# Hi tiles at 64 and lo tiles at 32 bytes modulo 128 from the weights, with the substitution's blocks zeroed earlier

## The chip, the cores and the metric

The kernel runs on one core of one Trainium2 chip. The metric is the device time of one execution, in microseconds (us); lower is better. One nanosecond (ns) is a thousandth of that. The engines are TensorE (PE; its weight loads are PEld), VectorE (DVE), ScalarE (ACT), GpSimd (POOL), and SyncE (SP), which here only issues DMA transfers. Each engine, and each issuing queue, works through its own instructions in program order.

## The reference

Two transformer blocks over 256 positions of width 1024, in float32. The part that the change touches is the first block's gated delta rule, whose chunked form needs the inverse of a unit lower triangular matrix for each of 16 pairs of chunk and head:

```python
def first_block(x, ...):
    h = rmsnorm(x, norm_mix_g[l]); proj = h @ w_in[l]
    y_a = short_conv_branch(bg, cg, xv, conv_a_w[l]) @ w_a_out[l]
    y_b = gdn_branch(q, k, v, z, a, b, ...) @ w_b_out[l]
    x = x + (sigmoid(ga) * y_a + sigmoid(gb) * y_b) @ w_o[l]
    x = x + conv_ffn(rmsnorm(x, norm_ffn_g[l]), w_up[l], ffn_conv_w[l], w_down[l])
    return rmsnorm(x, norm_final_g)

def gated_delta_rule_chunked(q, k, v, g, beta):
    decay = exp(where(tril, G[..., :, None] - G[..., None, :], -inf))   # G = cumsum(g)
    L = where(strict, einsum('bnhid,bnhjd->bnhij', k * beta, k) * decay, 0)
    sol = triangular_solve(eye + L, concat([v * beta, k * beta * exp(G)]), lower=True)
    ...                                            # state recurrence over the chunks

def second_block(x, ...):        # dilated attention and retention, gated; then
    x = x + square(relu(rmsnorm(x) @ w_up)) @ w_down
```

## The kernel before

Every dense product is made in three float32r matmuls. A float32 matrix is split into a hi part (rounded by ACT) and a lo part (the rest, subtracted by DVE); weights become the tiles `H` and `L`, the other operand a pair such as `Hh`, `Hl`. The product is hi·H + lo·H + hi·L (`dense`, line 334, which groups all products of one kind: eight matmuls with hi and `H`, eight with lo and `H`, eight with hi and `L`). In `fm_job` the weights are the loaded operand of 128 columns and the pair is the moving operand of 256 columns. In `tm_jobs` and `down2_job` it is the other way round: the pair is loaded, and 512 columns of weights move.

Weights come in jobs of 1 MB, loaded by SP into one of three `raw` buffers (line 316; three jobs ahead), and each job is two units. For unit n the program order is: one step of the running evacuations and side programs (`evs`, `auxes`; each is a Python generator, and a `yield` in it puts what follows it one unit later), the split of unit n+2 (`do_split`: ACT writes `H`, DVE writes `L`), then the matmuls of unit n, then another step of the side programs. So a side program's yields set where its instructions stand in the order of every engine.

Side programs that matter here: `gates` (a softplus series of small DVE operations on 16 columns) leads into `gdn_decay` (row sums on PE, then a decay matrix `gam`, broadcast from memory by two SP transfers, lines 501 and 502) and into `gdn_main`. There `U` is made and sent to memory (`scr`), and read back as 64 rows of 32x32 blocks (`blk` and `eb`, the two halves of tile `ebd`). `subst` inverts the blocks, 31 steps of two operations each, the first eight on DVE, the others on POOL, then writes the inverse and its transpose to memory, and scatters them back as diagonal blocks of `Em` and `Dm` (line 614, half from POOL's queue, half from SP's), tiles that must be zero elsewhere. `sub_ok` then lets `gdn_main` go on with the matmuls of line 663, which read `Dm` and `U`.

Where tiles lie: the pools are laid out one behind the other. `H` and `L` (4,096 bytes each) begin at multiples of 128 bytes. The 15 buckets of 8,192 bytes that hold all large tiles, hi and lo tiles among them, begin at a multiple of 128 too (`LINE_PAD` sees to it), and so do the four `mid` tiles (`mh`, `ml`) of the feed-forward parts. Taken modulo 256 the buckets' distance from `H` and `L` is 0 and that of the `mid` tiles is 128. Ahead of the first job stand dummy matmuls on zeros (`WARM`); they read the moving operand at 48, 56, 64 and 80 bytes (modulo 256) beyond the loaded one, eight matmuls each.

Of the kernel before, what the change touches and what calls it, by code (L numbers as in the profile page):

```python
# [7 lines left out]
F32R = mybir.dt.float32r  # L8
I32 = mybir.dt.int32
# [10 lines left out]
LINE_PAD = 8  # L20
HL_BUFS = 3
W_BUFS = 6
WARM = ([(0, 0, 512, 0)] * 11 + [(128 * i, 1024 + d, 256, i % 2) for d in (12, 14, 16, 20) for i in range(8)])
# [5 lines left out]
GAM_Y = 4  # L29
# [5 lines left out]
SC_Z = 4  # L35
# [63 lines left out]
def _build(tc, nc, A, ACT, DVE, POOL, PE, SP, raw_p, hl_p, c_p, b_p, t_p, m_p, s_p, d_p, x_p):  # L99
# [6 lines left out]
    free_tags = [f"b{i}" for i in range(N_BUCKETS)][::-1]  # L106
    tag_of = {}

    def alloc(shape, dt=F32, what="bk"):
        if not free_tags:  # L110
            raise RuntimeError(f"no bucket for {what} at {cur}: {len(tag_of)}")
        tag = free_tags.pop()
        t = b_p.tile([128] + list(shape), dt, tag=tag, name=nm(what))
        tag_of[id(t)] = (tag, t)
        return t

    def free(*ts):
        for t in ts:
            free_tags.insert(0, tag_of.pop(id(t))[0])
# [92 lines left out]
    cst("pad", [128, LINE_PAD])  # L212
# [31 lines left out]
    Hh = alloc([8, 256], F32R, "Hh")  # L244
# [184 lines left out]
    def gates():  # L429
# [123 lines left out]
    def gdn_main():  # L553
# [27 lines left out]
        def subst():  # L581
# [17 lines left out]
            gd["Em"], gd["Dm"] = alloc([16, 128], what="Em"), alloc([16, 128], what="Dm")  # L599
# [46 lines left out]
        rsqrt(rq, sq, 16, dve=True)  # L646
        rq2 = cst("rq2", [128, 16])
# [127 lines left out]
        Oh, Ol = alloc([8, 256], F32R, "Oh"), alloc([8, 256], F32R, "Ol")  # L775
# [42 lines left out]
    def bg_evac(p):  # L818
        def go(box):
            if p == 0:  # L820
                S["ya"] = (alloc([8, 256], F32R, "yah"), alloc([8, 256], F32R, "yal"))
# [160 lines left out]
    def up_evac(m, gate):  # L982
        def go(box):
# [16 lines left out]
            else:  # L1000
# [7 lines left out]
                mh = m_p.tile([128, 2, 256], F32R, tag="mh", name=nm("mh"))  # L1008
                ml = m_p.tile([128, 2, 256], F32R, tag="ml", name=nm("ml"))
# [325 lines left out]
    def ret_main():  # L1335
# [69 lines left out]
        orr = [(alloc([8, 256], F32R, "orh"), alloc([8, 256], F32R, "orl")) for _ in range(2)]  # L1405
# [128 lines left out]
    def up2_evac(m):  # L1534
        def go(box):
# [5 lines left out]
            mh = m_p.tile([128, 2, 256], F32R, tag="mh", name=nm("mh"))  # L1541
            ml = m_p.tile([128, 2, 256], F32R, tag="ml", name=nm("ml"))
# [123 lines left out]
```

## Time and profile before

| | |
|---|---|
| time, median of 3 runs (lowest, highest) | 1152.12 us (1150.99, 1152.6) |
| the profiled execution: its time, its span | 1150.97 us, 1149.2 us |
| granted TensorE clock, mean over the span | 0.991 of full speed |
| busy: PE, PEld, DVE, ACT, POOL | 98%, 93%, 65%, 51%, 21% |
| HBM read | 191.68 MB, 168 GB/s over the span |

The span runs from the first to the last instruction of the profiled execution; the time has 1.77 us more around it. Matmuls are pipelined: each lasts about 280 ns, but the next one starts long before it ends, so the rate of PE is read from the distance of starts, not from durations or the busy share. The granted clock has two levels, 2.4 GHz (1.00) and 1.2 GHz (0.50); a figure between them is a mean over a stretch.

### The profile page before, as it was taken

What the parts mean: (1) busy time and instruction counts of PE and PEld (TensorE: products, weight loads), DVE (VectorE), ACT (ScalarE), POOL (GpSimd) and SP (SyncE); (2) the same over time, 40 slices, a digit from 0 to 9 for tenths busy, and PEclk for the clock granted to TensorE, in tenths of its full rate; (3) what the DMA queues carried; (4) which work ended last, traced back from release to release, by engine and by line L of the source; (5) the groups of instructions that cost most, each with busy time, mean ns of one, the idle gap of its engine ahead of it and who ended that gap; (6) DMA issues with size and microseconds to landing.
All of it is one profiled execution on the core that took longest, in us unless ns stands there. A gap on an engine that the chain in (4) does not pass through costs nothing.

```text
span 1149.2 us, 20224 instructions
## 1 busy us (share of the span) xinstructions
PE 1127.2 (98%) x8340; PEld 1073.6 (93%) x8340; DVE 750.5 (65%) x1033; ACT 586.0 (51%) x944; POOL 241.7 (21%) x245
## 2 busy tenths in 40 slices
PE   9899897999999999999999999999999999999998
PEld 8899897999999999999878899889999999899997
DVE  4957984344577987778854566556685558655554
ACT  6776253256554444444678554555474445444442
POOL 2565696010401221222200500001340001000000
PEclk9999998999999999999999999999999999999999
DMA  8455366243554555555575544453436555555552
GB/s 258 147 164 186 111 193 174 75 146 112 182 186 150 181 188 183 192 178 178 183 250 190 184 146 147 139 191 113 163 129 220 184 184 168 176 191 189 190 187 74
DMA packets 155087, 194.82 MB, mean 170 GB/s; under 512 B 5678, under 2 KB 132005, under 8 KB 154740
## 3 DMA queue, kind: packets, MB, share of 16 engines
q1 hardware_dynamic: 153888, 191.57, 51.1%
q0 software_dynamic: 912, 1.43, 0.5%
q8 instruction: 65, 1.06, 0.4%
q10 hardware_dynamic: 196, 0.54, 0.1%
q14 instruction: 26, 0.21, 0.0%
HBM read 191.68 MB, written 1.84 MB: 168 GB/s over the span
## 4 chain that ended last, share of the span: by engine, by line
PE 84%; POOL 5%; DVE 4%; ACT 3%; DMA 2%; issue 2%; POOLq 0%; DVEq 0%; ACTq 0%
PE d L334 63%; PE x L334 13%; POOL bt L146 2%; POOL ebd L146 2%; DVE L L146 2%; ACT jk L143 1%; ACT H L143 1%; DVE w L149 1%; DMA Dm<-scr 1%; POOL gam L146 1%; PE x L663 0%; PE x L1181 0%; PE x L1206 0%; DMA scr<-U 0%; DMA xtm<-in_x_dram 0%
## 5 line engine op out<-in xcount | busy, mean ns | idle before, releaser
L146 DVE TENSOR_TENSOR L<-raw,H 128x1024 fp32r<-128x1024 f32 x354 | 443.2, 1258 | 256.8 <-ACT H L143 253.2
L143 ACT ACTIVATE H<-raw 128x1024 fp32r<-128x1024 f32 (+1 forms) x355 | 369.9, 1053 | 205.2 <-PE d L334 152.4
L334 PE MATMUL d<-Hh,L 128*128 128x256 f32 x576 | 82.2, 286 | 6.2 <-DVE L L146 6.2
L334 PE MATMUL d<-Hh,H 128*128 128x256 f32 x576 | 85.6, 292 | 0.7 <-ACT H L143 0.7
L334 PE MATMUL d<-nh,H 128*128 128x256 f32 x608 | 85.9, 283 | 0.0
L334 PE MATMUL d<-nl,H 128*128 128x256 f32 x608 | 85.7, 283 | 0.0
L334 PE MATMUL d<-nh,L 128*128 128x256 f32 x608 | 85.7, 283 | 0.0
L334 PEld LDWEIGHTS d<-Hh,L 128*128 128x128 f32 x576 | 74.7, 193 | 7.4 <-DVE L L146 7.4
L334 PE MATMUL d<-Hl,H 128*128 128x256 f32 x576 | 81.2, 284 | 0.0
L334 PEld LDWEIGHTS d<-nh,H 128*128 128x128 f32 x608 | 79.2, 191 | 1.2
L334 PEld LDWEIGHTS d<-nh,L 128*128 128x128 f32 x608 | 78.6, 192 | 0.0
L334 PEld LDWEIGHTS d<-nl,H 128*128 128x128 f32 x608 | 78.5, 192 | 0.0
L334 PEld LDWEIGHTS d<-Hh,H 128*128 128x128 f32 x576 | 75.2, 194 | 1.4 <-ACT H L143 0.9
L334 PEld LDWEIGHTS d<-Hl,H 128*128 128x128 f32 x576 | 74.9, 193 | 0.0
L334 PE MATMUL d<-H,x2h 128*128 128x512 f32 x208 | 56.9, 396 | 1.0 <-ACT H L143 1.0
L334 PE MATMUL d<-x2h,H 128*128 128x256 f32 x384 | 55.8, 288 | 0.0
L334 PE MATMUL d<-H,x2l 128*128 128x512 f32 x208 | 55.7, 390 | 0.0
L334 PE MATMUL d<-L,x2h 128*128 128x512 f32 x208 | 55.7, 390 | 0.0
L334 PE MATMUL d<-x2h,L 128*128 128x256 f32 x384 | 53.9, 283 | 0.0
L334 PE MATMUL d<-x2l,H 128*128 128x256 f32 x384 | 53.9, 283 | 0.0
L334 PEld LDWEIGHTS d<-x2h,H 128*128 128x128 f32 x384 | 49.8, 190 | 0.6
L334 PEld LDWEIGHTS d<-x2h,L 128*128 128x128 f32 x384 | 49.5, 191 | 0.0
(402 smaller groups left out, 1922.8 us busy)
## 6 DMA issues: line engine op xcount, KB each, us to landing
raw<-in_w_in_dram SPq DMA_DIRECT2D x86, 1024.0 KB, 5.1
raw<-in_w_up_dram SPq DMA_DIRECT2D x38, 1024.0 KB, 5.3
raw<-in_w_down_dram SPq DMA_DIRECT2D x27, 1024.0 KB, 4.8
raw<-in_w_proj_b_dram SPq DMA_DIRECT2D x8, 1024.0 KB, 5.1
raw<-in_w_a_out_dram SPq DMA_DIRECT2D x4, 1024.0 KB, 6.1
raw<-in_w_b_out_dram SPq DMA_DIRECT2D x4, 1024.0 KB, 5.3
raw<-in_w_o_dram SPq DMA_DIRECT2D x4, 1024.0 KB, 6.0
raw<-in_w_out_dram SPq DMA_DIRECT2D x4, 1024.0 KB, 5.2
```

Source lines behind the costliest of these rows:

```text
L143: ACT.activation(out=out, in_=in_, func=func, **kw)
L146: eng.tensor_tensor(out=out, in0=a, in1=b, op=op)
L149: DVE.scalar_tensor_tensor(out=out, in0=in0, scalar=scalar, in1=in1, op0=op0, op1=op1)
L334: PE.matmul(out, lhsT=x if swap else w, rhs=w if swap else x, start=first and ps == 0, stop=last and ps == group[-1] and group is (order o ...
```

## The change

Four of the 15 buckets become 8,320 bytes long, and hi tiles (`alloc_hi`) start 32 bytes into one of those. `LINE_PAD` goes, and small constants are reshuffled, so that every bucket starts 32 modulo 128 from the weights. Lo tiles and all else in buckets thus lie at 32, hi tiles at 64 modulo 128. Modulo 256 a hi tile lies at 64 or 192 beyond `H` and `L`, a lo tile at 32 or 160, depending on the bucket. `mh` and `ml` lie at 32 modulo 128 in the first block and at 0 in the second (`pair`). The dummy matmuls move at 32 or 64 instead of 48 to 80.

```diff
+    def alloc_hi(what):
+        tag, long, t = bucket(F32R, what, True)
+        v = t[:, 8 * long:8 * long + 2048].rearrange("p (a b) -> p a b", b=256)
...
+    def pair(what):
+        d = 24 * ("x2" in S)
+        return m_p.tile([128, 544], F32R, tag=what, name=nm(what))[:, d:d + 512].rearrange("p (a b) -> p a b", b=256)
...
-    cst("pad", [128, LINE_PAD])
...
-    Hh = alloc([8, 256], F32R, "Hh")
+    Hh = alloc_hi("Hh")                 # likewise x2h, nh, Oh, yah, mxh, orh, yh
```

`subst` allocates and zeroes `Em` and `Dm` at its head instead of behind the substitution. The two yields that stood there are gone, and `SC_Z` grows by two, so that line 663 stays at the unit where it was, while the scatter stands two units earlier.

```diff
-SC_Z = 4
+SC_Z = 6
...
-            for _ in range(3):
-                yield
+            gd["Em"], gd["Dm"] = alloc([16, 128], what="Em"), alloc([16, 128], what="Dm")
+            for k in ("Em", "Dm"):
+                POOL.memset(gd[k], 0.0)
+                yield
+            yield
...
-            POOL.memset(gd["Em"], 0.0)
-            yield
-            POOL.memset(gd["Dm"], 0.0)
-            yield
```

The softplus series gets two more yields and `GAM_Y` falls from 4 to 2: `gam` is made from row sums that stand two units later, and is read at the same unit as before. The reciprocal root `rq` on DVE, which ran as one block of nine small operations, is spread over three units:

```diff
-GAM_Y = 4
+GAM_Y = 2
...
-            if k in (2, 4):
+            if k in (1, 2, 4, 5):
...
-        rsqrt(rq, sq, 16, dve=True)
+        a = tmp("nw16", (16,))
+        DVE.tensor_scalar(out=rq.bitcast(I32), in0=sq.bitcast(I32), scalar1=-0.5, scalar2=float(0x5F3759DF), op0=MUL, op1=ADD)
+        for _ in range(3):
+            tt(DVE, a, rq, rq, MUL)
+            stt(a, a, -0.5, sq, MUL, MUL)
+            stt(rq, a, 1.5, rq, ADD, MUL)
+            yield
```

POOL's order at the end of the substitution, before (`scr` is memory, the DMA rows are issues on POOL's queue):

```order
L146 TENSOR_TENSOR ebd_1290<-ebd_1290,bt_1951 64x31
L600 DMA scr_1284<-ebd_1290 64x1024
L601 COPY ebd_1290<-ebd_1290 64x1024
L602 DMA scr_1285<-ebd_1290 64x1024
L603 MEMSET Em_1992 128x2048
L605 MEMSET Dm_1993 128x2048
L608 MEMSET P_2062 128x2048
L614 DMA Em_1992<-scr_1284 32x16x32 x2
L614 DMA Dm_1993<-scr_1285 32x16x32 x2
L146 TENSOR_TENSOR w_2094<-w_2094,w_2095 128x2x255
```

And POOL's order at the head of the substitution, of the change:

```order
L601 DMA ebd_1289<-scr_1282 64x1024
L604 MEMSET ebd_1289 64x1024
L605 MEMSET ebd_1289 64x32
L608 MEMSET Em_1341 128x2048
L608 MEMSET Dm_1342 128x2048
L168 TENSOR_TENSOR bt_1583<-ebd_1289 64x207
```

Two of the three memsets ahead of the scatter stand now between the read of the blocks and POOL's first step; the rest of POOL's order is the same.

SP's order around the scatter, before and then of the change (`raw` rows are weight loads of 1 MB):

```order
L316 DMA raw_2002<-in_w_in_dram 128x8x256
L316 DMA raw_2068<-in_w_a_out_dram 128x8x256
L614 DMA Em_1992<-scr_1284 32x16x32 x2
L614 DMA Dm_1993<-scr_1285 32x16x32 x2
L316 DMA raw_2146<-in_w_a_out_dram 128x8x256
```

```order
L337 DMA raw_2004<-in_w_in_dram 128x8x256
L633 DMA Em_1341<-scr_1283 32x16x32 x2
L633 DMA Dm_1342<-scr_1284 32x16x32 x2
L337 DMA raw_2075<-in_w_a_out_dram 128x8x256
L337 DMA raw_2145<-in_w_a_out_dram 128x8x256
```

The first load of `w_a_out` now stands behind the scatter instead of ahead of it.

DVE's order of the change where `rq` is made (`nw` and `grr` are its small operations, `keep` and `w` belong to the convolution, `L` is the split; before, all nine rows on `nw` and `grr` stood in one block ahead of `w`):

```order
L666 TENSOR_SCALAR grr<-gsum 128x16
L168 TENSOR_TENSOR nw_1700<-grr 128x16
L171 SCALAR_TENSOR_TENSOR nw_1700<-nw_1700,gsum 128x16
L171 SCALAR_TENSOR_TENSOR grr<-nw_1700,grr 128x16
L168 TENSOR_TENSOR w_1711<-d_1637,keep_1631 128x512
L175 TENSOR_SCALAR keep_1713<-w_1711,prm 128x256 x2
L168 TENSOR_TENSOR L_1717<-raw_1500,H_1716 128x1024
L171 SCALAR_TENSOR_TENSOR keep_1713<-w_1711,prm,keep_1713 128x255 x2
L171 SCALAR_TENSOR_TENSOR keep_1713<-w_1711,prm,keep_1713 128x254 x2
L168 TENSOR_TENSOR nw_1700<-grr 128x16
```

Six of the nine now stand behind the next `L`. PE's order differs only in the row sums of `gates`, which stand two units later.

## Rows read from the trace of the kernel before

**Rows 1.** The page: busy time of each engine (share of the span, instructions), and the engines' shares of the chain of work that ended last.

```profile
PE 1127.2 (98%) x8340; PEld 1073.6 (93%) x8340; DVE 750.5 (65%) x1033; ACT 586.0 (51%) x944; POOL 241.7 (21%) x245
PE 84%; POOL 5%; DVE 4%; ACT 3%; DMA 2%; issue 2%; POOLq 0%; DVEq 0%; ACTq 0%
```

**Rows 2.** PE in order of time, in steady stretches: start in us, time from the first start to the last end, line, operation, out<-moving and loaded operand, shape, count.

```profile
318.29 1.12 PE L334 MATMUL d<-Oh,H 128*128 128x256 f32 x8
...
328.85 1.12 PE L334 MATMUL d<-Oh,L 128*128 128x256 f32 x8
...
389.24 1.11 PE L334 MATMUL x<-mh,H 128*128 128x256 f32 x8
...
394.94 1.12 PE L334 MATMUL d<-nh,H 128*128 128x256 f32 x8
...
599.89 1.07 PE L334 MATMUL d<-H,x2h 128*128 128x512 f32 x4
...
610.77 1.07 PE L334 MATMUL d<-H,x2h 128*128 128x512 f32 x4
...
1000.84 1.10 PE L334 MATMUL x<-H,mh 128*128 128x512 f32 x4
...
1003.63 1.11 PE L334 MATMUL d<-nh,H 128*128 128x256 f32 x8
```

**Rows 3.** PE in order of time during the dummy matmuls, in stretches cut so that a row begins with the second of the eight at one distance (48, 56, 64 and 80 bytes in turn); then the first matmuls behind them, of which the last row is 16 transposes with 128 moving columns.

```profile
6.28 0.99 PE L271 MATMUL d<-warm 128*128 128x256 f32 x7
...
7.22 1.00 PE L271 MATMUL d<-warm 128*128 128x256 f32 x7
...
8.18 0.99 PE L271 MATMUL d<-warm 128*128 128x256 f32 x7
...
9.12 1.00 PE L271 MATMUL d<-warm 128*128 128x256 f32 x7
9.96 0.27 PE L250 MATMUL d<-cmats,prr 128*128 128x128 f32 x1
10.07 1.91 PE L282 MATMUL x<-cmats,jk 128*128 128x128 f32 x16
```

**Rows 4.** PE's groups by line, names and shape: count, busy us, mean ns of one, idle time before.

```profile
L334 PE MATMUL d<-nl,H 128*128 128x256 f32 x608 | 85.7, 283 | 0.0
L334 PE MATMUL d<-Hl,H 128*128 128x256 f32 x576 | 81.2, 284 | 0.0
L334 PE MATMUL d<-x2l,H 128*128 128x256 f32 x384 | 53.9, 283 | 0.0
L334 PE MATMUL d<-orl,H 128*128 128x256 f32 x128 | 18.0, 283 | 0.0
L334 PE MATMUL d<-yal,H 128*128 128x256 f32 x64 | 10.1, 307 | 0.0
```

**Rows 5.** The wait for the scatter. First, busy us (and count) of each engine by stretch, with the granted clock, the DMA share and GB/s; then PE in order of time, with the idle time before it and what ended it.

```profile
178.00:187.00 9.00, 1.48 (x13) 1.27 (x11) 2.06 (x4) 5.13 (x11) 6.25 (x8) 0.80 0.98 263
187.00:192.00 5.00, 4.60 (x21) 4.63 (x22) 5.00 (x7) 1.77 (x4) 4.13 (x2) 0.50 0.43 127
...
187.40 3.65 PE L663 MATMUL x<-Dm,U 128*128 128x64 f32 x16 [7.92 <-DMA Dm<-scr]
```

**Rows 6.** POOL in order of time around the substitution.

```profile
112.83 0.98 POOL L583 MEMSET ebd<- 64x1024 f32 x1
...
122.96 0.59 POOL L146 TENSOR_TENSOR bt<-ebd 64x207 f32<-64x207 f32 x1 [8.94 <-DVE ebd L146]
...
167.75 1.11 POOL L146 TENSOR_TENSOR ebd<-ebd,bt 64x31 f32<-64x31 f32 x1
...
172.69 1.82 POOL L603 MEMSET Em<- 128x2048 f32 x1
174.43 1.82 POOL L605 MEMSET Dm<- 128x2048 f32 x1
176.18 1.82 POOL L608 MEMSET P<- 128x2048 f32 x1
...
179.26 1.29 POOL L614 DMA_DIRECT2D Dm<-scr  x2
```

**Rows 7.** Transfers between 160 and 200 us (count, KB each, median us from issue to landing), and SP's queue in order of time.

```profile
raw<-in_w_a_out_dram SPq DMA_DIRECT2D x4, 1024.0 KB, 6.1
...
Dm<-scr POOLq DMA_DIRECT2D x2, 64.0 KB, 7.4
...
163.06 0.37 SPq L316 DMA_DIRECT2D raw<-in_w_a_out_dram  x1
174.54 0.88 SPq L614 DMA_DIRECT2D Em<-scr  x2
```

**Rows 8.** ACT's first instruction behind the stall, in order of time, with its idle time and what ended it.

```profile
181.87 0.63 ACT L143 ACTIVATE w<-w 128x512 f32<-128x512 f32 x1 [10.35 <-POOL w L146]
```

**Rows 9.** Two more stretches in which PE was short of work, in the columns of rows 5.

```profile
46.00:50.00 4.00, 1.73 (x14) 1.53 (x14) 3.90 (x8) 1.72 (x3) 1.42 (x2) 1.00 0.00 0
...
135.00:139.00 4.00, 1.60 (x14) 1.40 (x13) 3.90 (x8) 0.00 (x0) 3.69 (x5) 1.00 0.08 25
```

**Rows 10.** SP's issue of `gam`, and the first DVE operation that reads it.

```profile
58.47 0.34 SPq L502 DMA_DIRECT2D gam<-gs  x1
...
70.91 1.28 DVE L146 TENSOR_TENSOR gam<-gam,cmats 128x512 f32<-128x512 f32 x2
```

More of the change, by code (lines that the diff above doesn't have):

```diff
@@ L19 @@
 N_BUCKETS = 15
-LINE_PAD = 8
+N_LONG = 4
 HL_BUFS = 3
 W_BUFS = 6
-WARM = ([(0, 0, 512, 0)] * 11 + [(128 * i, 1024 + d, 256, i % 2) for d in (12, 14, 16, 20) for i in range(8)])
+WARM = ([(0, 0, 512, 0)] * 11 + [(128 * (i % 8), 1024 + (8 if i in (8, 9, 18, 19, 20, 21) else 16), 256, i % 2) for i in range(32)])
 NEG = -1.0e30
@@ L104, in nm, with bucket @@
         return f"{s}{uid[0]}"
-    free_tags = [f"b{i}" for i in range(N_BUCKETS)][::-1]
+    free_tags = {False: [f"b{i}" for i in range(N_BUCKETS - N_LONG)][::-1], True: [f"l{i}" for i in range(N_LONG)][::-1]}
     tag_of = {}
-    def alloc(shape, dt=F32, what="bk"):
[L110 to L115, printed above, removed]
+    def bucket(dt, what, long):
+        if not free_tags[long]:
+            long = not long
+        if not free_tags[long]:
+            raise RuntimeError(f"no bucket for {what} at {cur}: {[v[2] for v in tag_of.values()]}")
+        tag = free_tags[long].pop()
+        return tag, long, b_p.tile([128, 2080 if long else 2048], dt, tag=tag, name=nm(what))
+    def alloc(shape, dt=F32, what="bk"):
+        tag, long, t = bucket(dt, what, False)
+        n = int(np.prod(shape))
+        v = t[:, 0:n]
+        if len(shape) == 2:
+            v = v.rearrange("p (a b) -> p a b", b=shape[1])
+        elif len(shape) == 3:
+            v = v.rearrange("p (a b c) -> p a b c", b=shape[1], c=shape[2])
+        tag_of[id(v)] = (tag, long, what, v)
+        return v
+    def alloc_hi(what):
+        tag, long, t = bucket(F32R, what, True)
+        v = t[:, 8 * long:8 * long + 2048].rearrange("p (a b) -> p a b", b=256)
+        tag_of[id(v)] = (tag, long, what, v)
+        return v
+    def pair(what):
+        d = 24 * ("x2" in S)
+        return m_p.tile([128, 544], F32R, tag=what, name=nm(what))[:, d:d + 512].rearrange("p (a b) -> p a b", b=256)
     def free(*ts):
         for t in ts:
-            free_tags.insert(0, tag_of.pop(id(t))[0])
+            tag, long = tag_of.pop(id(t))[0:2]
+            free_tags[long].insert(0, tag)
     def tmp(tag, shape=(2, 256), dt=F32, bufs=None):
@@ L774, in gdn_main @@
         yield
-        Oh, Ol = alloc([8, 256], F32R, "Oh"), alloc([8, 256], F32R, "Ol")
+        Oh, Ol = alloc_hi("Oh"), alloc([8, 256], F32R, "Ol")
         while "z_ok" not in S:
@@ L820, in go @@
             if p == 0:
-                S["ya"] = (alloc([8, 256], F32R, "yah"), alloc([8, 256], F32R, "yal"))
+                S["ya"] = (alloc_hi("yah"), alloc([8, 256], F32R, "yal"))
             u = tmp("w", bufs=W_BUFS)
@@ L1007, in go @@
                     yield
-                mh = m_p.tile([128, 2, 256], F32R, tag="mh", name=nm("mh"))
-                ml = m_p.tile([128, 2, 256], F32R, tag="ml", name=nm("ml"))
+                mh = pair("mh")
+                ml = pair("ml")
                 split_act(mh, ml, md)
@@ L1026, in x2_evac @@
         free(*S["xf"])
-        S["x2"] = (alloc([8, 256], F32R, "x2h"), alloc([8, 256], F32R, "x2l"))
+        S["x2"] = (alloc_hi("x2h"), alloc([8, 256], F32R, "x2l"))
         oh, ol = S["x2"]
@@ L1404, in ret_main @@
             yield
-        orr = [(alloc([8, 256], F32R, "orh"), alloc([8, 256], F32R, "orl")) for _ in range(2)]
+        orr = [(alloc_hi("orh"), alloc([8, 256], F32R, "orl")) for _ in range(2)]
         def out_split(h):
@@ L1540, in go @@
             yield
-            mh = m_p.tile([128, 2, 256], F32R, tag="mh", name=nm("mh"))
-            ml = m_p.tile([128, 2, 256], F32R, tag="ml", name=nm("ml"))
+            mh = pair("mh")
+            ml = pair("ml")
             split_act(mh, ml, md)
```

9 lines of the change are left out of this document (4 added, 5 removed).

## The prediction

> **What bounds the kernel now.** I read the page's shares first: PE is busy 98% of the span and carries 84% of the chain of work that ended last; POOL comes next with 5% [rows 1]. So two things can move the time: the rate of matmuls, and the stretch in which PE waits for POOL's substitution.
>
> The rate I took from PE in order of time, as distance from start to start. With `Oh` moving, 88 matmuls of 256 columns (eleven groups of eight from 318.29) take 10.56 us, 120.0 ns each. The 16 transposes behind the dummy matmuls load 128 columns each as well and start (1.91 - 0.27)/15 = 109.3 ns apart [rows 3], so the load of weights alone does not set the 120. With `mh` moving, which lies 128 bytes elsewhere modulo 256, 48 take 5.70 us: 118.75 ns. With 512 columns of `H` moving, the twelve groups of four before 610.77 take 10.88 us, 226.7 ns each with `x2h` loaded; twelve matmuls with `mh` and `ml` loaded take 2.79 us, 232.5 ns [rows 2]. The same form of work goes at different rates, and place is one thing that differs between them, though order is another.
>
> The dummy matmuls show place by itself. From the second of eight at one distance to the second at the next: 0.94 us at 48 bytes (117.5 ns each), 0.96 at 56 (120.0), 0.94 at 64 (117.5); the last seven at 80 take 0.84 us (120.0) [rows 3]. Starts are given to 0.01 us, so each figure is good to 1.3 ns.
>
> The largest single stall is at 179 us: PE does 1.48 us of work in 9 us, then line 663 starts at 187.40, released by the scatter into `Dm`. The granted clock behind it is half, 0.50 from 187 to 192 [rows 5].
>
> **The change part by part: the substitution.** POOL ends the last step at 168.86, then writes, copies, and zeroes `Em`, `Dm` and `P`, three memsets of 1.82 us in a row, and only then issues the scatter [rows 6]. The `Dm` pieces from POOL's queue take 7.4 us to land [rows 7], which gives the release at 187.4. The change takes two of the three memsets out of this chain: 3.64 us. Their new place costs nothing: POOL has zeroed `ebd` by about 114.0 and then idles until 122.96, because DVE does the first eight steps; two memsets from 114.0 end at 117.7, with 5.3 us to spare [rows 6]. Without that cover they would be in the same chain and the gain would be nothing.
>
> Who else profits: ACT stood idle for 10.35 us because a convolution's addition was queued on POOL behind the memsets and the scatter [rows 8]. It too starts 3.64 us earlier, and with it the split of the unit behind line 663, so that unit does not become the next wait.
>
> SP's queue is what the change loads more. SP reached its scatter at 174.54; the load of `w_a_out` had gone ahead of it at 163.06 [rows 7]. Now this load waits behind SP's scatter. That scatter waits for the two writes to memory, not for memsets any more, so I expect it at about 172 and 175, and the load at about 176 instead of 163. With 6.1 us to land it is there at 182. ACT, whose first instruction behind the idle time moves from 181.87 to 178.2, has other work for some 2 us and then wants it, so the split is some 2 us late; PE wants it only behind the first 16 matmuls of line 663, which took 3.65 us [rows 5]. Hidden, with a margin of about 2 us.
>
> The chain may also begin earlier. DVE's small operations starved PE twice: from 46 to 50 us it was busy for 1.73 of 4 us, from 135 to 139 for 1.60 of 4, while DVE was busy for 3.90 in both [rows 9]. The change spreads these operations, so that six of the nine at the second place stand behind the next `L` instead of ahead of it. What PE wins at the second place, up to 2.4 us, is lost again in the wait at 179, since POOL's steps have begun by then and do not follow PE. What it wins at the first place, up to 2.3 us, comes ahead of the chain's begin and moves it, unless POOL's own queue holds it. Nothing to 3 us (with a little from faster matmuls); I take 1.5. Against it stands `gam`: issued at 58.47, read first at 70.91 [rows 10]. Two units of PE are some 6 us, so it is issued at about 65 and, at the 6.1 us of a 1 MB load [rows 7], lands at 71. That is just in time; a wait of up to 1 us on DVE is possible and is in that 1.5.
>
> Sum here: 3.64 + 1.5 = 5.1 us. Bounds: 2.6 (the memsets alone, and `gam` late by 1) and 8 (no stall left).
>
> **The matmuls.** Only those behind 190 us count, because the faster ones ahead of it run into the same wait. Lo parts moving over `H`: 608 + 576 + 384 + 128 in four families [rows 4], and 64 each in four smaller ones, of which `yal` is shown: 1,952. Ahead of 190 us stand 24 jobs of 16, that is 384. So 1,568 lo matmuls remain, and twice as many with hi, 3,136.
>
> Hi at 64 bytes: the dummy row says 117.5 against 120.0, 2.5 ns less [rows 2, 3]. The two starts are rounded, the eight are few and work on zeros, and two thirds of the hi tiles (`Hh`, `x2h`, the last `nh`) lie at 192 and not at 64 modulo 256, which no row shows. I take 2.0; bounds are nothing and 2.5. 3,136 x 2.0 = 6.3 us.
>
> Lo at 32 or 160: no row shows either. The nearest rows are 117.5 (48 and 64) and 120.0 (56, 80 and zero), so from nothing to 2.5 ns; in the middle, 1.2: 1,568 x 1.2 = 1.9 us. `mh` and `ml` in the first block move from 118.75 to a place with the same bounds: no change. Where 512 columns move, the second block's `mid` tiles fall half on distance zero and half on 128; if the 5.8 ns between the two rows of 512 columns come from place alone, half of 384 matmuls save 1.1 us. The 624 with `x2h` and `x2l` loaded go to places without a row; if they lose a third of that, 1.9 ns, it is 1.2 us. I set both against each other at nothing.
>
> Sum: 8.2 us. Of that I keep nine tenths, 7.4, since PE still waits here and there for splits that a faster PE meets sooner. Bounds: nothing, and 3,136 x 2.5 + 1,568 x 2.5 = 11.8.
>
> The Trainium skill speaks against this part. Its page "TensorE: Matmul & The Clock Gate" (Step-by-step: what each phase is for) says that PE has two independent SBUF read ports and that loading the next weights takes no read bandwidth from the running matmul; by it the place of a tile is indifferent and the sum would be 5.1 us alone. The rows disagree at least with the rate that goes with it (256 columns at 120.0 ns, against 109.2 by the formula of its section Back-to-back issue gap, an estimate), so I give that rival below less than the rows.
>
> **How it adds up.** 5.1 + 7.4 = 12.5 us. The profiled execution took 1150.97 us (1149.2 of span and 1.8 around it) and would take 1138.5. It was the fastest of the runs shown; against the median of 1152.1 the same sum gives 1139.6. I predict 1139.
>
> **The rivals.**
> - *Place does nothing.* If the difference in the dummy rows is rounding and the order of reads, the hi and lo matmuls stay at 120.0 and only the substitution gains: 1152 - 5 = 1147. For it: each dummy row has seven or eight matmuls. Against: `mh` at 118.75 over 48.
> - *Place does more.* If 32 bytes bring lo half-way to the transposes' 109.3, to 114.6 ns, lo gains 8.5 us instead of 1.9, and with a stall that vanishes the time is about 1130.
> - *The scatter eats its gain.* Three `raw` loads are now free to go in one run right behind SP's scatter, while POOL's scatter is under way. If its landing grows from 7.4 by the 3.64 us won, only the rest remains: about 1143.
> - *Slower.* A place can cost: 512 columns take 232.5 at one and 226.7 at another [rows 2]. If hi at 192 pays those 5.8 ns, the 2,100 or so such matmuls behind 190 us cost 12.2 us, against 5.1 and some 3.5 won elsewhere: 1155. It decides from about 4.1 ns per matmul on. No row of 256 columns lies above 120, which speaks against it.
>
> **How the numbers follow.** Chances: the forecast 0.62 (its own range 1133 to 1144), place does nothing 0.16, place does more 0.09, the scatter eats its gain 0.08, slower 0.05. The range of 1131 to 1147.5 leaves out the slower case, part of "does more" and the upper edge of "nothing". A change of under 0.2% (2.3 us) can't be told from none here. The second to fourth cases are all faster by more than that in their middle; with their edges: faster 0.91, same 0.05, slower 0.04.
>
> **What the profile of the change would show.** Groups of eight with hi moving start 0.94 us apart, with lo 0.95 (now 0.96 for both); if both stay at 0.96, the second term is wrong. On POOL one memset stands between the second write and the scatter, and two lie in the idle time behind 114 us; line 663 starts at about 182, released by the same scatter, and its wait is still some microseconds long with a half clock behind it, because PE arrives earlier. The stretch about 136 us shows no starved PE. The forecast fails if hi at 192 differs from hi at 64, if DVE's first steps slow down beside the two memsets, if the load of `w_a_out` lands behind 186 and becomes the wait, or if DVE waits for `gam`.

## The result and the profile after

| | before | after |
|---|---|---|
| time, median of 4 runs each, taken together | 1152.3 us | 1131.18 us (1129.97 to 1132.15) |
| ratio | | 0.9818 [0.9801, 0.9835] |
| the profiled execution: time, span | 1150.97, 1149.2 us | 1132.15, 1130.4 us |
| start of the matmuls that wait for `Dm` (line 663, now 688) | 187.40 us | 182.34 us |
| from there to the last start on PE | 957.5 us | 943.7 us |

The change wins 21 us, 1.8%. I had forecast 1139 us, with a range of 1131 to 1147.5; the time lies just inside its lower edge. In the profiled executions the span is 18.8 us shorter: 5.1 us lie ahead of the matmuls on `Dm`, as forecast, and 13.8 us behind them, where I had 7.4.

Line numbers behind the head of the file are 19 to 25 higher than before. From the page of the changed kernel, busy time and the chain that ended last, to hold against [rows 1]:

```profile
PE 1107.6 (98%) x8340; PEld 1051.7 (93%) x8340; DVE 755.6 (67%) x1033; ACT 584.9 (52%) x944; POOL 242.9 (21%) x245
PE 82%; POOL 4%; DVE 2%; ACT 2%; issue 1%; DMA 1%; DVEq 0%; ACTq 0%; POOLq 0%
```

The bound is the same: PE, busy for 98% of a shorter span. The wait for the scatter, to hold against [rows 5 to 7]: POOL in order of time; the transfers from 160 to 200 us (count, KB each, median us from issue to landing); SP's queue; the matmuls that wait; and two stretches (length, then busy time and count of PE, PEld, DVE, ACT, POOL, granted clock, DMA share, GB/s).

```profile
112.81 1.82 POOL L608 MEMSET Em<- 128x2048 f32 x1
114.56 1.82 POOL L608 MEMSET Dm<- 128x2048 f32 x1
121.70 0.59 POOL L168 TENSOR_TENSOR bt<-ebd 64x207 f32<-64x207 f32 x1 [5.32 <-DVE ebd L168]
...
167.42 1.18 POOL L168 TENSOR_TENSOR ebd<-ebd,bt 64x31 f32<-64x31 f32 x1
172.42 1.83 POOL L627 MEMSET P<- 128x2048 f32 x1
174.18 1.34 POOL L633 DMA_DIRECT2D Em<-scr  x2
175.51 1.29 POOL L633 DMA_DIRECT2D Dm<-scr  x2
...
Em<-scr POOLq DMA_DIRECT2D x2, 64.0 KB, 2.7
Dm<-scr POOLq DMA_DIRECT2D x2, 64.0 KB, 4.8
...
175.11 0.83 SPq L633 DMA_DIRECT2D Dm<-scr  x2
176.04 13.38 SPq L337 DMA_DIRECT2D raw<-in_w_a_out_dram  x4
...
182.34 3.65 PE L688 MATMUL x<-Dm,U 128*128 128x64 f32 x16 [6.65 <-DMA Dm<-scr]
185.75 2.06 PE L355 MATMUL d<-yah,H 128*128 128x256 f32 x8
...
178.00:187.00 9.00, 4.66 (x22) 4.69 (x23) 1.90 (x3) 5.07 (x10) 2.52 (x3) 0.62 1.05 323
187.00:192.00 5.00, 5.00 (x32) 5.00 (x32) 5.00 (x8) 3.52 (x6) 3.97 (x2) 0.66 0.54 172
```

The two memsets stand in POOL's idle time, as forecast, and one is left ahead of the scatter. PE still waits 6.65 us, and the granted clock about the wait is 0.62 and 0.66 on the mean, between the two levels (from 182 to 187 us it is 0.50, the lower one). The loads of `w_a_out` now stand behind SP's scatter and start at 176.04, half a microsecond after POOL's into `Dm`. POOL's scatters land faster than before: 2.7 and 4.8 us against some 7.4.

The rate of matmuls, to hold against [rows 2]: PE in order of time in two steady stretches.

```profile
330.80 1.07 PE L355 MATMUL d<-Oh,H 128*128 128x256 f32 x8
331.70 1.10 PE L355 MATMUL d<-Ol,H 128*128 128x256 f32 x8
332.64 1.08 PE L355 MATMUL d<-Oh,L 128*128 128x256 f32 x8
333.56 1.10 PE L355 MATMUL d<-mxh,H 128*128 128x256 f32 x8
334.50 1.10 PE L355 MATMUL d<-mxl,H 128*128 128x256 f32 x8
335.44 1.10 PE L355 MATMUL d<-mxh,L 128*128 128x256 f32 x8
336.38 1.10 PE L355 MATMUL d<-mxh,H 128*128 128x256 f32 x8
...
599.98 1.08 PE L355 MATMUL d<-H,x2h 128*128 128x512 f32 x4
600.90 1.10 PE L355 MATMUL d<-H,x2l 128*128 128x512 f32 x4
601.83 1.08 PE L355 MATMUL d<-L,x2h 128*128 128x512 f32 x4
```

With `Oh` and its neighbours moving, groups of eight started 0.96 us apart [rows 2]. Now `Oh` with `H` takes 0.90 us (112.5 ns each), `Ol` 0.94, `Oh` with `L` 0.92, and all three groups of `mx` 0.94. `Oh` lies 192 bytes modulo 256 beyond the weights, `mxh` 64. With 512 columns the groups of four take 0.92 and 0.93 us, against (610.77 - 599.89)/12 = 0.907 before.

Summed from start to start over all matmuls behind the wait (what exceeds 130 ns, or 245 with 512 columns, is put down as idle; "`x2h`, `x2l` loaded" and "`mid` loaded" are the two kinds with 512 moving columns):

| matmuls behind the wait | count | ns before | ns after | won, us | forecast, us |
|---|---|---|---|---|---|
| hi moving | 3,136 | 120.1 | 116.7 | 10.7 | 6.3 |
| lo moving | 1,568 | 120.1 | 117.4 | 4.3 | 1.9 |
| `mid` tiles and `oab` moving | 624 | 118.9 | 117.0 | 1.2 | 0 |
| 512 columns, `mid` loaded | 383 | 232.4 | 230.0 | 0.9 | 0 |
| 512 columns, `x2h`, `x2l` loaded | 624 | 228.0 | 231.5 | -2.2 | 0 |
| idle and the rest | | | | -1.1 | -0.8 |
| sum | | | | 13.8 | 7.4 |

By place, the 1,920 hi matmuls at 192 bytes went from 120.0 to 115.7 ns, the 1,216 at 64 from 120.1 to 118.1 (modulo 256, as all distances here).

### The profile page after: what moved, and what is told of

It reads as the page before. It is cut to its first block, busy times and chain, and to the rows that moved or that the text cites. A ratio compares the mean times of both kernels' runs of the same rounds, so it can differ in the third digit from the quotient of the medians.

```text
span 1130.4 us, 20225 instructions
## 1 busy us (share of the span) xinstructions
PE 1107.6 (98%) x8340; PEld 1051.7 (93%) x8340; DVE 755.6 (67%) x1033; ACT 584.9 (52%) x944; POOL 242.9 (21%) x245
## 4 chain that ended last, share of the span: by engine, by line
PE 82%; POOL 4%; DVE 2%; ACT 2%; issue 1%; DMA 1%; DVEq 0%; ACTq 0%; POOLq 0%
PE d L355 61%; PE x L355 13%; POOL ebd L168 2%; POOL bt L168 2%; DVE L L168 1%; ACT H L165 1%; DMA Dm<-scr 1%; ACT jk L165 1%; PE x L688 0%; PE x L1206 0%; PE x L1231 0%; PE x L690 0%; ACT w L165 0%; PE x L1265 0%; PE x L691 0%
## 5 line engine op out<-in xcount | busy, mean ns | idle before, releaser
L355 PE MATMUL d<-Hh,L 128*128 128x256 f32 x576 | 79.7, 281 | 8.0 <-DVE L L168 8.0
L355 PE MATMUL d<-Hh,H 128*128 128x256 f32 x576 | 81.6, 284 | 0.7 <-ACT H L165 0.7
L355 PEld LDWEIGHTS d<-Hh,L 128*128 128x128 f32 x576 | 72.1, 188 | 10.1 <-DVE L L168 10.0
L355 PEld LDWEIGHTS d<-Hh,H 128*128 128x128 f32 x576 | 71.7, 188 | 1.1 <-ACT H L165 1.0
L355 PEld LDWEIGHTS d<-Hl,H 128*128 128x128 f32 x576 | 72.5, 188 | 0.0
L165 ACT ACTIVATE w<-w 128x512 f32<-128x512 f32 (+1 forms) x35 | 21.7, 619 | 53.2 <-POOL w L168 22.0
```

The source lines that it names most:

```text
L165: ACT.activation(out=out, in_=in_, func=func, **kw)
L355: PE.matmul(out, lhsT=x if swap else w, rhs=w if swap else x, start=first and ps == 0, stop=last and ps == group[-1] and group is (order o ...
```

## The experiments

The theory after the result: the change has two parts that add up, places (13.8 us) and substitution (5.1), and the place term was too small because hi at 192 runs faster than the row at 64 from which I took it. Rivals: the substitution wins more than line 663 shows; the spreading of DVE's operations does it.

Every run stood beside the kernel before, and "less" and the ratios are against that. Its median was 1150.93 us for the first three runs, 1152.11 for all at 192, all at 64 and hi alone, 1152.18 for the two with hi at 192 and lo at 160 or 32, and 1151.18 for the last two. The two runs with many dummy matmuls are single executions, read for the rates alone.

**Places alone.** The kernel before with the tiles of the change; `subst`, its yields and DVE's operations as before. Since tiles are then allocated in another order, five lo tiles fall into other buckets than in the change: `Ol`, `mxl`, one of the two `orl` and the last `nl` lie at 32 instead of 160, `yl` at 160 instead of 32. All hi tiles lie as in the change.

> The kernel before with the new places alone (hi tiles, lo tiles, the `mid` tiles and the dummy matmuls as in the change); the zeroing, the waits and DVE's small operations stand as before. Theory of places: the 13.7 us that the changed kernel wins behind line 663 come from matmuls that start closer together, so this kernel wins them whole: 1152.3 - 13.7 = 1138.6 us, from 1137 to 1140, and line 663 starts near 187 as before. My forecast's own sizes (2.0 ns for hi, 1.2 for lo, nine tenths of it) give 1152.3 - 7.4 = 1145. Rival that the substitution wins more than the 5 us by which line 663 moved: also about 1145, and the next kernel then shows more than 7 us.

Measured: 1136.2 us, ratio 0.9872 [0.9857, 0.9886], 14.7 us less. Behind the wait it takes 941.9 us, 15.6 less than before; the wait ends 0.9 us later, at 188.27. Places carry some seven tenths of the gain. Of the 1.8 us more than the change wins behind the wait, 1.4 are in hi (116.2 ns on average, against 116.7): `mxh`, at 64 in both kernels, takes 117.8 ns beside `mxl` at 160 and 113.9 beside `mxl` at 32.

**The substitution alone.** The kernel before with

```diff
-            for _ in range(3):
+            gd["Em"], gd["Dm"] = alloc([16, 128], what="Em"), alloc([16, 128], what="Dm")
+            for k in ("Em", "Dm"):
+                POOL.memset(gd[k], 0.0)
                 yield
+            yield
...
-            POOL.memset(gd["Em"], 0.0)
-            yield
-            POOL.memset(gd["Dm"], 0.0)
-            yield
...
-SC_Z = 4
+SC_Z = 6
```

> The kernel before with the substitution's part alone: `Em` and `Dm` zeroed at its head, two units' longer wait. All tiles lie as before. If the memsets alone move line 663, it starts 3.64 us earlier, at about 183.8, and the time is 1152.3 - 3.6 = 1148.7 us; with the 5.1 us seen in the changed kernel from this part alone it would be 1147.2. If the rest of the 5.1 us came from faster matmuls or from DVE's spreading ahead of the chain, 1148.7. If the substitution carries what the matmul term does not, under 1145.

Measured: 1146.95 us, ratio 0.9967 [0.9953, 0.9981], by the ratio 3.8 us less (2.2 to 5.4). This interval holds both 3.6 and 5.1, so the time alone does not tell which of them is right; the trace does. POOL's scatter and the matmuls behind it, in order of time, with the transfers from 160 to 200 us between them:

```profile
175.05 1.29 POOL L612 DMA_DIRECT2D Dm<-scr  x2
...
Dm<-scr POOLq DMA_DIRECT2D x2, 64.0 KB, 5.1
...
182.27 3.65 PE L661 MATMUL x<-Dm,U 128*128 128x64 f32 x16 [3.52 <-DMA Dm<-scr]
```

The scatter is issued 4.2 us earlier, of which the memsets are 3.5 (POOL's last step ends 0.7 us earlier here); from its issue to the first matmul it takes 7.2 us instead of 8.1. With places alone, where two loads of `w_a_out` are issued just ahead of POOL's scatter as before (SP issues them at 177.32 and 177.86, POOL its scatter into `Em` from 178.05 and that into `Dm` from 179.38), it took 8.9. So line 663 starts 5.1 us earlier by this part alone, with no faster matmul and no spreading. The two parts together, 14.7 + 3.8 = 18.5 us, come within their intervals to the 19.7 us that the next run wins beside the same kernel before.

**Without the spreading.** The changed kernel with `if k in (2, 4)`, `GAM_Y = 4` and `rsqrt(rq, sq, 16, dve=True)` again.

> The changed kernel without the spreading of DVE's small operations (the two extra pauses, `GAM_Y` and the three pauses in the root of the queries' norms are as before). If the spreading wins the up to 1.5 us that I gave to an earlier start of the chain, this kernel takes 1131.2 + 1.5 = 1132.7 us and line 663 starts 1.5 us later, at about 183.8. If the spreading only trades one stall for several (the changed kernel has new ones of 1.0 to 1.4 us at 52, 72 and 76 us), 1131.2 within 0.7 us, or even less.

Measured: 1131.2 us, ratio 0.9827 [0.9812, 0.9841], 19.7 us less, the same as the change (0.9818). Line 663 starts at 181.42, earlier rather than later. What the spreading does can be read in the changed kernel: stretches (columns as above; the third row is the kernel before, in the stretch of the second), then DVE's wait for `gam` and its splits, then PE behind them.

```profile
46.00:50.00 4.00, 3.57 (x31) 3.57 (x31) 3.97 (x8) 3.17 (x7) 1.69 (x2) 1.00 0.63 188
135.00:141.00 6.00, 3.54 (x30) 3.34 (x30) 5.86 (x11) 0.00 (x0) 5.47 (x7) 1.00 0.00 0
...
135.00:141.00 6.00, 3.60 (x24) 3.40 (x23) 5.89 (x10) 0.00 (x0) 5.50 (x7) 0.84 0.05 17
...
70.36 1.29 DVE L168 TENSOR_TENSOR gam<-gam,cmats 128x512 f32<-128x512 f32 x2 [2.77 <-DMA gam<-gs]
71.57 2.06 DVE L168 TENSOR_TENSOR L<-raw,H 128x1024 fp32r<-128x1024 f32 x1
...
73.69 1.21 PE L355 MATMUL d<-Hh,L 128*128 128x256 f32 x8 [0.87 <-DVE L L168]
77.97 1.20 PE L355 MATMUL d<-Hh,L 128*128 128x256 f32 x8 [1.20 <-DVE L L168]
```

The stall at 46 us is nearly gone (PE busy 3.57 of 4 us, against 1.73 in [rows 9]), but `gam`, issued at 65.50 instead of 58.47, makes DVE wait 2.77 us, and PE loses 0.87 and 1.20 us that it had not lost. About 137 us PE is short of work as before: it is busy for 3.54 of 6 us, against 3.60, and DVE for 5.86, against 5.89.

**A sweep of distances.** The kernel before with dummy matmuls on zeros (extra work at the head):

```diff
+WARM = ([(0, 0, 512, 0)] * 11
+        + [(128 * (i % 8), 1024 + d, 256, i % 2) for d in list(range(0, 64, 4)) + list(range(60, -1, -4)) for i in range(24)]
+        + [(1024 + 128 * (i % 6) + d, 512 * (i % 2), 512, 0) for d in range(0, 64, 4) for i in range(12)])
```

> The kernel before with many more dummy matmuls at its start: 256 columns moving, 24 at each distance of moving from loaded tile, 0 to 240 bytes in steps of 16, once upward and once downward; then 512 columns moving, 12 at each distance. Its whole time is longer by those matmuls, about 135 us, and is of no interest. If the distance modulo 256 alone sets the rate, both passes give one figure for each distance: 120 ns at 0, 118.75 at 128, 117.5 at 48 and 64, some 117 at 32 and 160, some 114 at 192; and for 512 columns some 227 at 0 and 230 to 232 elsewhere. If the distance counts modulo 128 only, 64 and 192 agree. If what went before decides (two states at one distance), the two passes differ.

PE in order of time, one distance in each row (112 and 192 bytes on the way up, 64 and 0 on the way down, 24 matmuls of 256 columns each):

```profile
25.76 2.88 PE L273 MATMUL d<-warm 128*128 128x256 f32 x24
39.85 2.89 PE L273 MATMUL d<-warm 128*128 128x256 f32 x24
82.31 2.99 PE L273 MATMUL d<-warm 128*128 128x256 f32 x24
93.61 3.04 PE L273 MATMUL d<-warm 128*128 128x256 f32 x24
```

The last one of a row lasts some 0.27 us, so the 23 distances are 113.5, 113.9, 118.3 and 120.4 ns. From the single starts, once a group has settled (from the ninth on; from the third with 512 columns), in ns:

| moving beyond loaded, bytes mod 256 | 0 | 16 | 32 | 48 | 64 | 80 | 96 | 112 | 128 | 144 | 160 | 176 | 192 | 208 | 224 | 240 |
|---|---|---|---|---|---|---|---|---|---|---|---|---|---|---|---|---|
| 256 columns, upward | 120.0 | 118.7 | 116.9 | 118.3 | 117.7 | 119.7 | 119.9 | 113.3 | 118.7 | 118.7 | 117.3 | 119.1 | 113.3 | 119.1 | 118.5 | 116.9 |
| 256 columns, downward | 120.0 | 116.5 | 117.8 | 118.2 | 117.8 | 119.7 | 119.9 | 114.5 | 118.7 | 118.7 | 118.7 | 119.1 | 113.3 | 118.9 | 118.5 | 117.1 |
| 512 columns | 228.0 | 226.9 | 233.6 | 233.3 | 228.9 | 229.9 | 232.7 | 233.8 | 233.8 | 233.3 | 234.3 | 232.2 | 233.1 | 233.2 | 233.6 | 226.7 |

So place alone changes the rate of matmuls that are otherwise the same, over 113.3 to 120 ns, and 227 to 234 with 512 columns. The figures are those of the real ones: 120 at 0, 118.7 at 128 (`mh`), 113.4 for `Oh` at 192, 233 for `x2l` loaded. By the Trainium skill's page "TensorE: Matmul & The Clock Gate" (Step-by-step: what each phase is for), loading weights takes no read bandwidth from the running matmul; if nothing else set the rate, place would be indifferent, and this table shows that it is not. What makes one distance slower than another no run shows. Small differences between the two passes (16, 32, 160) say that history counts too; at 112 the group on the way down ran at 113.3 as well, but only from its twelfth matmul on.

One rival the sweep leaves: the loaded tile stood at one place modulo 256 while the moving one was shifted, so the place of the moving tile by itself would explain the 256 columns as well as the distance. The dummy matmuls ahead of the other runs speak for the distance. There the tile that they read begins elsewhere. In the two runs below with all at 192, and with hi at 192 and lo at 32, the moving operand that is 64 bytes from the loaded one lies where the sweep has 0 and 96, which took 120 ns; there it settles at 118 in the one, at 113 and 118 in the other, the rates that 64 has elsewhere.

**All at 192, all at 64.** The changed kernel with buckets of one length, padded so that every hi and lo tile lies at one distance (and the `mid` tiles at 192, or half at 64 and half at 192):

```diff
-N_LONG = 4
+N_LONG = 0
+LINE_PAD = 8
...
+    cst("pad", [128, LINE_PAD])
```

with 40 instead of 8 for distance 64.

> The changed kernel with every moving tile (hi, lo, `mid`) at 192 bytes modulo 256 beyond the loaded weights, by 32 bytes of padding ahead of the buckets and without long buckets. Nothing else is changed. If the sweep of dummy matmuls holds for the real ones (113.9 ns at 192, against 117.1 for lo at 32 or 160 and 117.8 for hi at 64; with 512 columns 228.5 where loaded tile and moving tile stand so, against 233.1 for `x2l` now): 1,568 lo x 3.2 + 1,240 hi x 3.9 + 528 mids x 3.2 + 208 x 4.6 + 384 x 0.8 ns = 5.0 + 4.8 + 1.7 + 1.0 + 0.3 = 12.8 us less, 1118.4 us. If something else than the distance held the lo parts back (their order behind hi, the other bucket), the hi and 512 terms alone stay: 1125. If the low gaps of hi at 192 belong to the tiles and not to the place, 1131 as now.

> The same with every hi and lo tile at 64 bytes modulo 256 (the `mid` tiles half at 64, half at 192): the same place modulo 128 as in the run beside it, other modulo 256. If the distance counts modulo 256: against the changed kernel 1,928 hi behind 190 us lose 3.3 ns (6.4 us), 1,568 lo lose 0.7 (1.1), 416 matmuls of 512 columns with `x2h` loaded lose some 3 (1.2): 1131.2 + 8.7 = 1139.9 us, about 21 us above the run at 192. If it counts modulo 128, as the change's own words have it, both runs take the same time.

Measured: all at 192 takes 1131.59 us, 0.9826 [0.9808, 0.9843], no better than the change: the expectation of 1118.4 failed. All at 64 takes 1136.52 us, 0.9874 [0.9857, 0.9892], 3.4 us better than expected. Why, PE in order of time shows in the run at 192:

```profile
301.05 1.07 PE L357 MATMUL d<-Hl,H 128*128 128x256 f32 x8
301.95 1.08 PE L357 MATMUL d<-Hh,L 128*128 128x256 f32 x8
302.86 0.60 PE L810 MATMUL x<-cmats,o 128*128 128x128 f32 x4
303.22 1.19 PE L357 MATMUL d<-Hh,H 128*128 128x256 f32 x8
304.24 1.10 PE L357 MATMUL d<-Hl,H 128*128 128x256 f32 x8
305.19 1.11 PE L357 MATMUL d<-Hh,L 128*128 128x256 f32 x8
...
332.01 1.11 PE L357 MATMUL d<-mxh,H 128*128 128x256 f32 x8
332.95 1.10 PE L357 MATMUL d<-mxl,H 128*128 128x256 f32 x8
```

Ahead of four short matmuls a group of `Hl` takes 0.90 us (gaps of 113, 113, 114 ns in turn); behind them the same group at the same distance takes 0.95 (117, 118, 118, 119), and this lasts, over `Oh`, `mx` and `nh`, for hundreds of matmuls. So at one distance PE has two modes, 113.4 and 117.7 ns, and keeps the one into which the last disturbance put it. At 64 there are both too (in the run at 64 `x2h` takes 116.4 on average, with groups at 113 and at 118). The theory that the distance alone decides is gone.

**Hi alone.** The changed kernel with `LINE_PAD = 56`, an offset of 16 columns in the long buckets instead of 8, and `mid` tiles 512 wide, so that lo and `mid` lie at 0 or 128.

> The changed kernel with the hi tiles where it puts them and the rest back at 0 or 128 modulo 256 (lo and `mid` tiles). By the sweep lo goes from 117.1 to 118.5 (some 860 of those behind 190 us) and 119.7 (some 700), the 528 mids from 117.1 to 119.7, `x2l` loaded from 233.1 to 228.8: + 1.2 + 1.9 + 1.4 - 1.1 = 3.4 us, 1134.6. So of the 13.7 us behind line 663 the hi term is some 10 and the lo term with the mids some 3.4. With my forecast's sizes lo alone would be 1.9 and hi 6.3; if lo carries the part that I did not forecast, this kernel takes 1138 or more.

Measured: 1133.98 us, 0.9845 [0.9829, 0.986]. Hi keeps 10.1 us of its gain. Lo runs at 118.4 ns, against 120.1 before and 117.4 in the change, so 1.6 of its 4.3 us come from 32 and 160 instead of 0 and 128. The other 2.7 have two halves. The 864 lo matmuls that the long buckets move from 0 to 128 take 118.7 ns, 1.3 us less; that is the sweep's figure for 128, so their own place explains it. The 704 that still lie at 0 take 118.1 and not 120.0: 1.4 us that come from their neighbours, groups of hi that are no longer at 0.

**Pairs.** The kernel before with dummy matmuls, eight at a, eight at b, eight at a, four times, with three short ones ahead of the first and the third time (extra work at the head).

> The kernel before with dummy matmuls in the order of the real ones: eight of 256 columns at a distance a, eight at b, eight at a, four times for each pair (three short matmuls ahead of the first and the third time), a = 64, 192 and 112 bytes, b = eleven distances from 0 to 240. Its whole time, about 370 us longer, is of no interest. The run with all tiles at 192 has shown two modes at one place: groups of eight at 113.4 ns, and from some point on groups at 117.7 for hundreds of matmuls. If a mode lasts until something disturbs it, a uniform pair (192, 192) keeps the mode that it begins with, and pairs with b = 32 or 160, whose own gaps go up and down by 3 to 7 ns, bring a = 192 back to 113.4 within three matmuls each time and leave a = 64 at 117.7. If the modes are chance, groups at a differ from one time to the next within one pair. A pair in which both a and b run at 113.4 would make the kernel faster by 3.7 ns for each lo matmul.

The group at a that follows directly on one at a (means of eight, two values) and the groups at b (lowest to highest of four):

| a, b | a behind a | b |
|---|---|---|
| 192, 192 | 117.8, 117.9 | 117.8 to 117.9 |
| 192, 160 | 117.8, 117.6 | 117.9 to 119.2 |
| 192, 32 | 113.4, 113.4 | 117.0 to 117.6 |
| 64, 160 | 117.8, 117.6 | 116.9 to 117.5 |
| 64, 32 | 113.4, 113.4 | 117.8 to 119.6 |
| 112, 112 | 113.4, 113.4 | 113.2 to 115.5 |

These pairs give the same both times, so what went before decides; of all 33 pairs two (192 with 64, and with 112) gave one mode the first time and the other the second. A b of 32 brings 192 and 64 into the fast mode, 160 does not, against the expectation for 192, and a uniform 192 kept the slow one that the short matmuls left. With all at 112 the settled groups ran at 113.4; no kernel with its own tiles there was run.

**All hi at 192, all lo at 160 or 32.** The changed kernel with the buckets laid out in one row, the four for hi last, shifted by `HI_OFF` columns:

```diff
+    for k in [f"b{i}" for i in range(N_BUCKETS - N_LONG)] + [f"l{i}" for i in range(N_LONG)]:
+        b_p.tile([128, 2048 + HI_OFF * (k == "l0")], F32, tag=k, name="pre_" + k)
```

> The changed kernel with all hi tiles at 192 bytes modulo 256 (it has a third of them at 64) and all lo tiles at 160 (it has some of them at 32); the `mid` tiles as in the change. In the changed kernel `Oh` at 192 with `Ol` at 160 runs 113.4, 117.4 and 114.2 ns in turn, `mxh` at 64 with `mxl` at 160 117.8, 117.1 and 117.7. If the uneven gaps of lo bring hi back into its fast mode each time, and 64 is the place where they do not, then 1,240 hi matmuls win some 4.0 ns: 1131.2 - 5.0 = 1126.2 us. If the mode is not tied to the pair of places (the dummy pair of 192 and 160 stayed at 117.7), hi can come out at 117.7 here: 1,928 x 3.3 = 6.4 us more than the change, 1137.6, or anything between.

> The same with all lo tiles at 32 bytes. In the changed kernel `Hh` at 192 with `Hl` at 32 runs about 113.5, 117 and 115.5 ns in turn; the dummy pair of 192 and 32 ran 113.4, 117.0 and 115.5, the only pair with 192 whose groups in the middle stayed at 113.4 each time beside 0 and 96. If the pair decides, all families run so: against the changed kernel 620 hi behind lo gain 2.3 ns and 620 gain 4.3, `Oh`, the last `nh` behind their lo lose 1.3 over some 300: 1131.2 - 4.1 + 0.4 = 1127.5 us. If not, 1131 to 1138.

Measured: lo at 160 gives 1130.63 us, 0.9812 [0.9795, 0.9828]; lo at 32 gives 1128.83 us, 0.9796 [0.9781, 0.981]. Their intervals overlap, with each other and with the change's, so what follows is read from the rates in the profiles, not from the times. PE in order of time, first with 160, then with 32:

```profile
330.75 1.10 PE L358 MATMUL d<-Ol,H 128*128 128x256 f32 x8
331.69 1.10 PE L358 MATMUL d<-Oh,L 128*128 128x256 f32 x8
332.63 1.11 PE L358 MATMUL d<-mxh,H 128*128 128x256 f32 x8
333.58 1.11 PE L358 MATMUL d<-mxl,H 128*128 128x256 f32 x8
```

```profile
331.05 1.10 PE L359 MATMUL d<-Ol,H 128*128 128x256 f32 x8
331.98 1.09 PE L359 MATMUL d<-Oh,L 128*128 128x256 f32 x8
332.91 1.07 PE L359 MATMUL d<-mxh,H 128*128 128x256 f32 x8
333.81 1.10 PE L359 MATMUL d<-mxl,H 128*128 128x256 f32 x8
334.75 1.09 PE L359 MATMUL d<-mxh,L 128*128 128x256 f32 x8
335.67 1.07 PE L359 MATMUL d<-mxh,H 128*128 128x256 f32 x8
```

With lo at 160, `Oh` runs at 117.8 ns for its whole family, at the places at which it ran at 113.4 in the changed kernel: this pair holds either mode. With lo at 32 the groups of `Oh`, `mxh`, `orh` and `yh` with `H` come back to 113.4, each time anew (those with `L`, right behind lo, take 115.5); `x2h` (116.1) and `yah` (116.2) do so only in part. Hi lies at the same places in both runs; for these four families it is the place of the *other* tile that decides its mode.

**Together, and the change again on the same chip.** The last kernel with `mh` of the first block at 192 as well, and without the spreading.

> What the runs so far point to, together: all hi tiles at 192 and all lo at 32 (as in the run before this), `mh` of the first block at 192 too, and DVE's small operations as in the kernel before, without the spreading that won nothing. `mh` gains some 3 ns on 352 matmuls, 1.1 us; line 663 starts up to 1 us earlier. 1128.8 - 1.1 = 1127.7 us, or 1126.7 with the earlier start; about 0.3 to 0.4% below the changed kernel on the same chip. If hi at 192 falls into its slow mode here, 1131 to 1136.

> The changed kernel itself on the same chip, to compare with: 1131.2 us.

Measured: 1129.24 us, 0.9809 [0.9794, 0.9824], and 1130.39 us, 0.9823 [0.9809, 0.9837]. The intervals overlap: a gain of 0.1% that can't be told from none. Behind the wait the first takes 939.6 us against 942.7, but its wait ended at 183.58 against 181.65. The end of the wait moves between executions too (182.34 and 181.65 in the two profiles of the changed kernel), by less than this.

All runs but the two with many dummy matmuls, means from start to start behind the wait, in ns (reckoned as in the table above; `mid` here without `oab`):

| kernel | hi | lo | `mid` | 512, `x2` | 512, `mid` | us behind the wait |
|---|---|---|---|---|---|---|
| before | 120.1 | 120.1 | 118.7 | 228.0 | 232.4 | 957.5 |
| substitution alone | 120.0 | 120.1 | 118.7 | 227.9 | 232.4 | 957.4 |
| places alone | 116.2 | 117.3 | 117.0 | 231.5 | 230.0 | 941.9 |
| the change | 116.7 | 117.4 | 117.0 | 231.5 | 230.0 | 943.7 |
| the change again | 116.6 | 117.3 | 117.0 | 231.6 | 230.0 | 942.7 |
| without the spreading | 116.7 | 117.4 | 117.0 | 231.5 | 230.0 | 943.2 |
| hi alone | 116.8 | 118.4 | 119.9 | 230.9 | 227.5 | 945.2 |
| all at 192 | 117.1 | 116.7 | 117.8 | 230.0 | 229.8 | 943.2 |
| all at 64 | 117.7 | 117.6 | 115.5 | 233.6 | 231.4 | 947.7 |
| hi 192, lo 160 | 116.4 | 118.1 | 117.2 | 231.8 | 230.0 | 944.7 |
| hi 192, lo 32 | 115.6 | 117.2 | 117.1 | 231.5 | 230.1 | 940.4 |
| together | 115.5 | 117.2 | 115.2 | 231.6 | 230.1 | 939.6 |

## Why the prediction came out right, step by step

**Direction and mechanism: right.** Both terms are there and add up. That the time lies in the range, by 0.2 us, is luck in part: the matmul term, 13.8, lies above the upper bound of 11.8 that I had given it, and the lower edge of the range was reached only because it allowed more for the other term than that one won. The rival that place does nothing is refuted by the run with places alone, the slower rival by the same run, and by the sweep, in which no place of 256 columns is above 120 ns. Of the rival that place does more, the time came out (about 1130) and the reason did not: it had lo at 114.6 ns, and lo takes 117.4; the surplus is in hi.

**The substitution, 5.1 us: right in its sum, wrong in one of its two parts.** The memsets gave 3.5 us from POOL's last step to the scatter (10.40 us before, 6.91 after), where I had 3.64; they last 1.82 us each but start 1.75 apart [rows 6]. The 1.5 us that I put down to an earlier begin of the chain, from DVE's spreading, did not come from there: POOL's last step ended 0.26 us earlier in the profiled change, and the run without the spreading takes the same time. That the sum is 5.1 all the same is luck. What came in its place is a faster landing, from issue to the first matmul 6.83 us instead of 8.14. That is my rival "the scatter eats its gain" with its sign turned: I had seen that the loads of `w_a_out` move behind SP's scatter, and thought that they would run beside POOL's; they are now issued behind the start of that too. That the loads are the cause is likely, not shown. POOL's scatter into `Dm` landed after 6.5 to 8.2 us (median of its two pieces) in the four profiles with two loads issued just ahead of it (before, places alone, the two with dummy matmuls), and after 4.8 to 5.8 in the ten with the loads behind. From issue to the first matmul the ranges overlap: 7.3 to 8.9 us with the loads ahead, 6.8 to 8.3 behind. Moving the loads alone was not tried.

**`w_a_out`: right that it is hidden, wrong on its size.** ACT waited for it until 184.02, not 182, and the unit behind the wait began at 185.75 without idle time all the same.

**`gam`: under-sized.** I allowed 1 us on DVE; it was 2.77, and two stalls of PE. The runs show no time lost by it, nor any won at 46 us: the run without the spreading is as fast, and POOL's last step ended at 167.67 us there, at 168.60 and 166.95 in the two profiles of the change.

**The stretch at 136 us: wrong.** I said that no starved PE would be seen there. DVE has 5.9 us of work in these 6 us whatever the order, so the later `L` only became late by other operations.

**The matmul term, 7.4 us: mis-sized; it measured 13.8.** Counts were right (3,136 and 1,568). Hi won 3.4 ns, not 2.0, lo 2.7, not 1.2. The step that failed is the price of hi at 192. I took it from the dummy row at 64 bytes, which shows the slow mode, and cut it to 2.0. At 64 that is what hi won; at 192 it won 4.3 (120.0 to 115.7), since there it runs at 113.4 ns for part of the time. I had named "hi at 192 differs from hi at 64" as what would break the forecast, but priced it only as a loss. The bound of 2.5 ns was no bound: one row at one distance does not bound another distance. Of lo's 4.3 us, where I had 1.9, some 2.9 can be its own place by the run with hi alone, and the other 1.4 come from its neighbours, which the prediction did not think of. `mid` and `oab`, which I had at nothing, won 1.2 us. With 512 columns the loss at `x2` was 2.2 us, where I had weighed 1.2 against a gain of 1.1 (0.9 measured).

## What to carry to other kernels

Where PE is the bound and the weights change with every matmul, look at the distance from start to start, not at the busy share, and try where the moving tile lies relative to the loaded one modulo 256 bytes: here 16 distances gave 113 to 120 ns, and a padding of some bytes won 1.3% of the kernel. Measure a whole row of distances with dummy matmuls first, but in the order of the real ones, since a rate found alone need not be the one that the same tile has between its neighbours. When work is moved out of a chain, look too at which transfers it now comes ahead of: here a faster landing gave 1.3 us beside the 3.5 of the work, though its cause is not shown.

## What the runs showed that I had not expected

PE keeps a rhythm: at 64 and at 192 bytes the same matmuls run at 113.4 or at 117.7 ns, settle within some three to twelve matmuls, and stay for hundreds until short matmuls or a tile at another distance disturb them. Giving all tiles one of the two best places of the sweep (all at 192) was therefore worth nothing (1131.59 us against 1131.18), while a neighbour at a worse one (lo at 32, 117 ns) brought four families of hi back to 113.4 each time. Two things stay open: why a distance has the rate that it has, and what else chooses the mode. In the changed kernel `yh` at 64 beside `yl` at 32 ran at 117.6, where the dummy pair of 64 and 32 ran at 113.4. And the order of instructions is not all: the last dummy matmuls ahead of the first job, at 64, are the same at the same places in the change and in the run without the spreading, and their profiles show 113 ns in the one and 118 in the other.
